# Routing into the experts of a hybrid layer: rows gathered without their norm, a weight slot as landing place, an embedding product cut in half groups, and a shorter overflow handler

## The chip, the cores and the metric

The kernel runs on one core of one Trainium2 chip. The time of a run is the device time in microseconds (us) of that core; runs are compared by their median. TensorE is called PE in the rows, VectorE DVE, ScalarE ACT, GpSimd POOL, and the queue of SyncE, which issues nearly all transfers, SP.

## The reference

One decoder layer on 512 tokens of width 1,024, all in float32. What matters here is its second half:

```python
x = x + hybrid_mixer(rms_norm(x, g_mix), ...)          # x1 in this text
h = rms_norm(x, g_moe)                                 # x1 * rstd * g_moe
# hier_moe(h): best of 4 groups, then the best 2 of its 4 experts
for e in range(16):
    hid = silu(t @ w_gate[e]) * (t @ w_up[e])          # t = h, 1024 -> 512
    y = y + combine[:, e:e + 1] * (hid @ w_down[e])    # 512 -> 1024
x = x + y
x = x + sigmoid(rms_norm(x, g_ple) @ w_ple_gate) * (p @ w_ple_proj)
```

Each expert has three float32 matrices of 2 MB. `p @ w_ple_proj` is the embedding; it depends on nothing that the layer computes, so it can be done anywhere before the end.

## The kernel before

Matrix products are taken in three parts: weights and activations are each split into a high part `hi` (ACT casts it) and a low part `lo` (DVE subtracts), and PE adds up hi·hi, hi·lo and lo·hi. A class `Stream` feeds the weights: loads of 1 MB go to "slots" (tags `raw0` to `raw4`, six more in `ringb`, and `x0`, `x1`, which first hold the residual stream), each slot is split in two steps into one of six pairs of hi/lo tiles, and a slot whose second half has been split is handed back (`W.give`), whereupon SP issues the next load into it. So SP runs ahead of PE by as many loads as there are free slots.

The experts work on gathered rows. Every expert has room for CAP = 96 tokens. In the last part of the mixer (`out_proj(t, 1)`, for four blocks `t` of 128 tokens) each block is squared (`square0`, `square1`), POOL raises the mean to the power -1/2 (`rs_moe`), DVE writes `h2 = x1 * rstd * g_moe` (`norm_moe`, L862), and SP stores it to the DRAM tensor `h2d` (L864). Router logits are made on PE from the transposed x1 (`x1_tr`, `logits`), compared on DVE (`route`), and turned into a place in each expert's list by a product with a triangular matrix (`rank`). A product of the one-hot matrix with `vals` (`slots`) gives the list of token numbers `toki`, the rows for the result `rowi` and the weights `sw`. For experts 0 and 1 this is done in two steps, first the list (columns 0 and 1 of `vals`), later the weight (columns 2 to 4, three bfloat16 parts of one float32), since the weights take longer (`weights`, `weights2`).

Then POOL gathers the rows of expert 0 into `xe[0]` and of expert 1 into `xe[1]` by an indirect transfer out of `h2d` (`gather`, L1060); PE transposes them (`transposed`, L1078), ACT and DVE split them (L1069, L1070), and the stream of expert products starts (`stream_mm`, `mm3`, L1103): for each expert gate (`pg`), up (`pu`) and down (`pd`). `silu` (L1125) and `times_up` (L1145) stand between them. The result rows are scaled by `sw` and added to the DRAM tensor `xd` by an indirect transfer (`scatter`, L1117).

The embedding is worked off beside the routing: eight groups `ple(i)` of six matmuls each (L804), with a copy out by ACT (`ple_out`, L812), are put by hand between the routing's steps. Order on each engine is the order of the program. Groups 0 to 2 lie before the gather, 3 to 5 behind it, 6 and 7 behind the transposes of expert 0.

After the gate product of expert 0 stands `overflow`: each engine loads the size of the fullest expert into a register (L1152) and jumps over a handler if it is at most 96 (L1153). With these inputs the handler is never entered. Its code is a loop over the 16 experts, with the 5 further portions of 96 tokens written out one after the other inside it.

Lines in the rows: L98 is the load of a weight slot by SP, L112 and L113 are `hi` and `lo` of `Stream.split`, L875 the logits' scaling, L917 the product in `slots`, L922 `toki`, L962 to L973 `weights2`.

Of the kernel before, what the change touches and what calls it, by code (L numbers as in the profile page):

```python
# [151 lines left out]
def hymba_layer(ctx, tc, x, p, g_mix, w_in, w_gla_gate, b_gla_gate, g_gla_out, w_conv, w_out,  # L152
# [18 lines left out]
    h2d = dram.tile([S, D], F32, name="h2d")  # L171
# [41 lines left out]
    vals = consts.tile([P, NT, NE, 5], BF16, name="vals")  # L213
# [60 lines left out]
    rows = mc.tile([P, P], F32, name="rows")  # L274
# [519 lines left out]
    def ple(i):  # L794

        t, ci = divmod(i, 2)
        if i == 0:
            for _ in range(2):
                wp.extend(W.take())
        pps_[i] = pp = mm_ps(f"pp{t}_{ci}")  # L800
        for k in range(2):
            (xh, xl), (wh, wl) = pT[k], wp[k]
            for n, (a, b_) in enumerate(((xh, wh), (xh, wl), (xl, wh))):
                pe.matmul(pp, a[:, tok(t)], b_[:, half(ci)], start=(k + n == 0), stop=(k == 1 and n == 2))  # L804
        if i == 7:
            W.done(2)
            W.give(pTt[0][0])
# [30 lines left out]
    x1T, h2, s2m, rs_moe = {}, {}, {}, {}  # L838
# [29 lines left out]
    def logits(t, ks=range(NK)):  # L868
# [5 lines left out]
        if NK - 1 in ks:  # L874
            ve.scalar_tensor_tensor(lg[:, t, :], pl[:, :20], rs_moe[t], brt, op0=OP.mult, op1=OP.add)  # L875
# [32 lines left out]
    sw = rtp.tile([CAP, NE], F32, name="sw", bufs=1)  # L908
# [3 lines left out]
    def slots(e, oh, vals, toki, rowi, sw, name, c0=0, c1=5, fill=False):  # L912
# [13 lines left out]
        if c1 == 5:  # L926
# [154 lines left out]
    for e in range(2):  # L1081
        gather(xe[e][:CAP], col(toki, e))
# [377 lines left out]
```

## Time and profile before

| | |
|---|---|
| median of three runs (lowest, highest) | 628.27 us (627.46, 628.48) |
| the profiled execution's own time | 629.62 us |
| its span, from first to last instruction | 627.9 us |
| mean granted clock of TensorE | 0.982 |
| busy: PE, DVE, ACT, POOL | 95%, 76%, 58%, 19% |
| DMA, mean over the span | 236 GB/s |

All positions below are us from the start of the span. The time lies 1.7 us over the span; the profiled execution is 1.35 us slower than the median. A PE that is reported busy is not a PE at its peak, since its matmuls overlap.

### The profile page before, as it was taken

Reading aid. Unit: us, or ns where it says so; the run is one execution under the profiler, and the core shown is the slowest. Engines: PE = TensorE matmul, PEld = TensorE weight load, DVE = VectorE, ACT = ScalarE, POOL = GpSimd, SP = SyncE. Lnnn points to the kernel's source line nnn. Section 1 sums busy time; section 2 is a strip of 40 time slices with the busy share of each in tenths; the row PEclk is TensorE's granted clock in tenths of the full one; section 3 lists DMA queues with packets and bytes.
Section 4 is the critical chain, followed back from the end, with each engine's and each line's share of the span. In section 5 each row is a group of like instructions: output and inputs, shape, how many; then the busy total and the mean of one; then the engine's idle time right before and its main releaser. Section 6 shows DMA issues by size and latency. Waiting matters only on the chain.

```text
span 627.9 us, 8404 instructions
## 1 busy us (share of the span) xinstructions
PE 594.7 (95%) x3006; PEld 453.8 (72%) x3006; DVE 479.6 (76%) x808; ACT 364.6 (58%) x516; POOL 121.9 (19%) x148
## 2 busy tenths in 40 slices
PE   7999999999999999559999999999999999988995
PEld 6897888887778787447777777777777777656784
DVE  4643799863593668359999999999999988879863
ACT  4532646103732342438788798777887977776332
POOL 1440654000700002002222222112222210100012
PEclk8999999999999999779999999999999999999998
DMA  8622221240129685776999999999999999986001
GB/s 274 207 102 68 101 68 67 68 135 1 67 68 331 239 316 224 256 264 234 356 356 353 368 368 356 354 354 350 354 347 362 367 340 363 369 256 260 34 34 67
DMA packets 73007, 148.45 MB, mean 236 GB/s; under 512 B 4797, under 2 KB 5396, under 8 KB 72942
## 3 DMA queue, kind: packets, MB, share of 16 engines
q1 hardware_dynamic: 69054, 136.69, 60.8%
q0 software_dynamic: 3744, 10.89, 7.6%
q8 instruction: 26, 0.43, 0.3%
q10 hardware_dynamic: 160, 0.27, 0.1%
q14 instruction: 23, 0.19, 0.1%
HBM read 137.56 MB, written 12.71 MB: 239 GB/s over the span
## 4 chain that ended last, share of the span: by engine, by line
PE 43%; DMA 6%; DVE 3%; ACT 2%; issue 1%; POOLq 0%; DVEq 0%; ACTq 0%
PE pu L1103 12%; PE pd L1103 11%; PE pg L1103 11%; PE pgate L1103 5%; DMA raw<-in_w_exp_down_dram 3%; DMA x<-in_w_exp_down_dram 2%; DMA x<-in_w_exp_up_dram 2%; DVE lo L113 1%; PE pt_xT L1078 1%; ACT hi L112 1%; PE pgate_last L1413 1%; DVE lo L118 1%; PE pt_hT L1078 1%; PE px L1310 1%; PE pz L1229 0%
## 5 line engine op out<-in xcount | busy, mean ns | idle before, releaser
L113 DVE TENSOR_TENSOR lo<-raw,hi 128x1024 fp32r<-128x1024 f32 x172 | 204.1, 1218 | 21.5 <-ACT hi L112 20.3
L112 ACT CAST hi<-raw 128x1024 fp32r<-128x1024 f32 x172 | 171.7, 1049 | 6.2 <-DMA raw<-in_w_exp_down_dram 4.9
L1060 POOL DMA_INDIRECT xe<-h2d,toki x16 | 27.9, 1741 | 200.9 <-PE pt_xT L1078 160.4
L118 DVE SCALAR_TENSOR_TENSOR lo<-raw,cst,hi 128x512 fp32r<-128x512 f32 (+1 forms) x52 | 41.9, 850 | 17.9 <-ACT hi L117 17.7
L113 DVE TENSOR_TENSOR lo<-x,hi 128x1024 fp32r<-128x1024 f32 x30 | 36.2, 1219 | 5.7 <-ACT hi L112 5.6
L1117 POOL DMA_INDIRECT xd<-ye,rowi x15 | 29.9, 1992 | 51.0 <-ACT ye L1271 47.4
L117 ACT ACTIVATE hi<-raw,cst 128x512 fp32r<-128x512 f32 (+1 forms) x52 | 34.0, 717 | 0.7 <-DMA raw<-in_w_in_dram 0.7
L112 ACT CAST hi<-x 128x1024 fp32r<-128x1024 f32 x30 | 30.9, 1050 | 2.1 <-DMA x<-in_w_exp_down_dram 1.8
L1103 PE MATMUL pg<-hi,xT_1h 128*96 128x512 f32 x60 | 24.5, 408 | 0.0
L1103 PE MATMUL pu<-hi,xT_0h 128*96 128x512 f32 x60 | 24.4, 407 | 0.0
L1103 PE MATMUL pu<-lo,xT_1h 128*96 128x512 f32 x60 | 23.8, 396 | 0.0
L1103 PE MATMUL pg<-hi,xT_1l 128*96 128x512 f32 x60 | 23.8, 396 | 0.0
L1103 PE MATMUL pu<-hi,xT_0l 128*96 128x512 f32 x60 | 23.8, 396 | 0.0
L1103 PE MATMUL pu<-hi,xT_1l 128*96 128x512 f32 x60 | 23.8, 396 | 0.0
L1103 PE MATMUL pg<-lo,xT_1h 128*96 128x512 f32 x60 | 23.7, 395 | 0.0
L1103 PE MATMUL pg<-hi,xT_0h 128*96 128x512 f32 x60 | 23.7, 395 | 0.0
L1103 PE MATMUL pg<-lo,xT_0h 128*96 128x512 f32 x60 | 23.7, 395 | 0.0
L1103 PE MATMUL pu<-lo,xT_0h 128*96 128x512 f32 x60 | 23.7, 395 | 0.0
L1103 PE MATMUL pg<-hi,xT_0l 128*96 128x512 f32 x60 | 23.7, 394 | 0.0
L1103 PE MATMUL pu<-hi,xT_1h 128*96 128x512 f32 x60 | 23.7, 394 | 0.0
L728 POOL TENSOR_TENSOR xs<-xs,sg 128x128 f32<-128x128 f32 x16 | 11.3, 736 | 44.2 <-ACT sg L723 44.1
L636 ACT ACTIVATE sq<-xs 128x512 f32<-128x512 f32 x4 | 2.5, 632 | 28.5 <-DVE xs L618 28.5
(539 smaller groups left out, 1583.9 us busy)
## 6 DMA issues: line engine op xcount, KB each, us to landing
raw<-in_w_exp_gate_dram SPq DMA_DIRECT2D x30, 1024.0 KB, 12.8
raw<-in_w_exp_down_dram SPq DMA_DIRECT2D x26, 1024.0 KB, 9.9
raw<-in_w_exp_up_dram SPq DMA_DIRECT2D x25, 1024.0 KB, 15.3
raw<-in_w_in_dram SPq DMA_DIRECT2D x10, 1024.0 KB, 5.1
x<-in_w_exp_up_dram SPq DMA_DIRECT2D x7, 1024.0 KB
x<-in_w_exp_down_dram SPq DMA_DIRECT2D x6, 1024.0 KB, 17.2
xs<-in_x_dram SPq DMA_DIRECT2D x16, 256.0 KB, 5.4
raw<-in_w_out_dram SPq DMA_DIRECT2D x4, 1024.0 KB
```

Source lines behind the costliest of these rows:

```text
L112: self.nc.scalar.copy(hi, rw)
L113: los.append(lambda: eng.tensor_sub(lo, rw, hi.bitcast(F32)))
L117: self.nc.scalar.activation(hi[:, c_], rw[:, c_], AF.Copy, scale=g_)
L118: los.append(lambda c_=c_, g_=g_: eng.scalar_tensor_tensor(lo[:, c_], rw[:, c_], g_, hi[:, c_].bitcast(F32), op0=OP.mult, op1=OP.subtract))
L636: se.activation(osq[c], to[c], AF.Square)
L728: ge.tensor_tensor(tv, tv, sgs[i][:, tok(t)], op=OP.mult)
L1060: ge.indirect_dma_start(out=x_, out_offset=None, in_=h2d, in_offset=bass.IndirectOffsetOnAxis(ap=idx, axis=0), bounds_check=S - 1, oob_is_ ...
L1078: pe.transpose(pt[:, k * n:(k + 1) * n], src[:n, tok(k)], ident[:n, :n])
L1103: pe.matmul(dst, a, b_, start=(k + n == 0), stop=(k == nk - 1 and n == 2))
L1117: ge.indirect_dma_start(out=xd, out_offset=bass.IndirectOffsetOnAxis(ap=idx, axis=0), in_=y_, in_offset=None, bounds_check=S + P - 1, oob_ ...
L1310: pe.transpose(pt[:, tok(k)], X(t)[:, ci * HALF + k * P:ci * HALF + (k + 1) * P], ident)
L1413: pe.matmul(pgl[i][:, :256], a, b_[:, 256 * i:256 * i + 256], start=(k + n == 0), stop=(k == NK - 1 and n == 2))
```

## The change

Five things. (1) The rows stored for the gather are `x1 * g_moe` without the reciprocal root (`gained`, into `xgd`), so they need no square, no power and no norm; they are stored one half row block at a time, the first half while the mixer still runs. The reciprocal root goes along as three more bfloat16 columns of `vals` (`norms`), comes out of `slots` as `sw[:, e, 1]`, and is applied in `silu` (its scale) and `times_up` (now a scalar_tensor_tensor). (2) Expert 0's rows land in the weight slot `x0`, which is handed back after they have been transposed; `x1` alone is freed beforehand. (3) The embedding runs in 16 half groups of three matmuls; 0 to 6 lie before the lists of tokens, 7 to 10 behind the gathers, 11 to 15 before the transposes, which therefore come after the whole embedding and, on DVE, after `norms` and `weights2`. (4) The lists of experts 2 and 3 are clamped as those of 0 and 1 were (`fill`), so that all 96 rows are gathered. (5) In the handler the 5 portions become an inner loop.

```diff
-    h2d = dram.tile([S, D], F32, name="h2d")
+    xgd = dram.tile([S, D], F32, name="xgd")
-    vals = consts.tile([P, NT, NE, 5], BF16, name="vals")
+    vals = consts.tile([P, NT, NE, 8], BF16, name="vals")
...
-    def ple(i):
-
+    def ple(j):
+
+        i, k = divmod(j, 2)
         t, ci = divmod(i, 2)
...
+        if k == 0:
+            pps_[i] = mm_ps(f"pp{t}_{ci}")
+        (xh, xl), (wh, wl) = pT[k], wp[k]
+        for n, (a, b_) in enumerate(((xh, wh), (xh, wl), (xl, wh))):
+            pe.matmul(pps_[i], a[:, tok(t)], b_[:, half(ci)], start=(k + n == 0), stop=(k == 1 and n == 2))
+        if k:
+            ple_out(i)
...
-    def norm_moe(t):
-        for i in range(2):
-            ve.scalar_tensor_tensor(h2[t][i], X(t)[:, half(i)], rs_moe[t], gmoe[:, half(i)],
-                                    op0=OP.mult, op1=OP.mult)
-            sy.dma_start(h2d[tok(t), half(i)], h2[t][i])
+        ge.tensor_tensor(rsm[:, t:t + 1], m, neghalf, op=OP.pow)
+
+    def gained(t, i):
...
+        ve.tensor_mul(xg[t, i], X(t)[:, half(i)], gmoe[:, half(i)])
+        sy.dma_start(xgd[tok(t), half(i)], xg[t, i])
...
+    def norms():
+
+        r3 = rtp.tile([P, NT, 3], BF16, name="r3", bufs=1)
+        for j in range(3):
+            ve.tensor_copy(r3[:, :, j], rsm)
+            if j < 2:
+                ve.tensor_tensor(rsm, rsm, r3[:, :, j], op=OP.subtract)
+        ve.tensor_copy(vals[:, :, :, 5:8], r3[:, :, None, :].to_broadcast([P, NT, NE, 3]))
...
     lo0 = W.split(later=True)
+    ple(0)
     x1_tr(t, 1)
     square1(t)
-    lo0()
-    ple(0)
-    norm_moe(t)
+    gained(t, 1)
     for u in range(2, NT):
         sy.dma_start(xd[tok(u)], X(u))
+    lo0()
+    ple(1)
+    ple(2)
     logits(t, range(4, NK))
     lo1 = W.split(later=True)
-    ple(1)
-    ple_out(0)
-    ple(2)
+    for j in range(3, 6):
+        ple(j)
     route(t)
-    ple_out(1)
     rank(t)
+    ple(6)
+    for e in range(2):
+        slots(e, oh01[e], vals, toki, rowi, sw, f"{e}", 0, 2, fill=True)
...
-    for e in range(2):
-        gather(xe[e][:CAP], col(toki, e))
-    W.free += [(ring, f"x{i}") for i in range(2)]
+
+    x0 = ring.tile([P, 2 * D], F32, tag="x0", name="xe_0")
+    gather(x0[:CAP, :D], col(toki, 0))
+    gather(xe[1][:CAP], col(toki, 1))
+    W.free.append((ring, "x1"))
     W.load()
-    for i in range(3, 6):
-        ple(i)
+    for j in range(7, 11):
+        ple(j)
     weights()
-    for i in range(3, 6):
-        ple_out(i)
     se.preload_act_table_set("silu_and_others")
+    norms()
     lo2()
-    xT = transposed(xe[0][:, half(0)], "xT0a") + transposed(xe[0][:, half(1)], "xT0b")
-    for i in range(6, 8):
-        ple(i)
-        ple_out(i)
     weights2()
+    for j in range(11, 16):
+        ple(j)
+    xT = transposed(x0[:, half(0)], "xT0a") + transposed(x0[:, half(1)], "xT0b")
+    W.give((ring, "x0"))
...
-        se.activation(sgs[e][:CAP], pgs[e][:CAP], AF.Silu)
+        se.activation(sgs[e][:CAP], pgs[e][:CAP], AF.Silu, scale=sw[:, e, 1:2])
...
-            slots(e, oh[e], vals, toki, rowi, sw, f"{e}")
+            slots(e, oh[e], vals, toki, rowi, sw, f"{e}", fill=(e < 4))
...
-        ve.tensor_mul(sgs[e][:CAP], sgs[e][:CAP], pus[e][:CAP])
+        ve.scalar_tensor_tensor(sgs[e][:CAP], pus[e][:CAP], sw[:, e, 1:2], sgs[e][:CAP], op0=OP.mult, op1=OP.mult)
...
-                for rep in range(1, -(-S // CAP)):
-                    kb = rt.tile([P, NT], F32, name="kb")
-                    ve.tensor_scalar(kb, ke, float(-CAP * rep), None, op0=OP.add)
+                with tc.For_i(1, -(-S // CAP), 1):
+                    ve.tensor_scalar(ke, ke, float(-CAP), None, op0=OP.add)
...
+    def first_weights():
+        for e in range(2):
+            slots(e, oh01[e], vals, toki, rowi, sw, f"{e}", 2, 8)
...
-    stream_mm(pgs[0][:CAP], xTs[0], NK, {3: lambda: silu(0)})
-    for e in range(2):
-        slots(e, oh01[e], vals, toki, rowi, sw, f"{e}", 2, 5)
+    stream_mm(pgs[0][:CAP], xTs[0], NK, {2: first_weights, 3: lambda: silu(0)})
```

## Rows read from the trace of the kernel before

**Rows 1.** Chain that ended last, in order of time (start, length, what)

```profile
285.73 2.85 PE pg L1103 x12
...
321.74 2.79 PE pg L1103 x12
...
489.99 17.53 DMA raw<-in_w_exp_down_dram
```

**Rows 2.** Windows: stretch, length, busy time of engines, PEclk, DMA share, GB/s

```profile
240.00:252.00 12.00, 10.73 (x64) 8.53 (x64) 10.55 (x36) 5.24 (x10) 4.33 (x3) 1.00 0.62 239
252.00:262.00 10.00, 3.65 (x15) 3.15 (x15) 2.22 (x9) 3.01 (x5) 0.00 (x0) 0.76 1.03 334
262.00:268.00 6.00, 6.00 (x24) 4.34 (x23) 3.19 (x8) 3.88 (x5) 0.00 (x0) 0.83 0.44 148
268.00:276.00 8.00, 2.55 (x18) 1.80 (x16) 4.97 (x10) 3.65 (x5) 0.00 (x0) 0.89 1.04 382
276.00:288.00 12.00, 10.92 (x51) 7.76 (x52) 6.76 (x19) 4.75 (x6) 1.93 (x1) 0.79 0.31 101
288.00:300.00 12.00, 12.00 (x64) 8.62 (x63) 11.63 (x20) 10.00 (x14) 4.70 (x2) 1.00 0.91 321
...
360.00:480.00 120.00, 120.00 (x592) 85.20 (x592) 112.54 (x160) 98.02 (x122) 23.84 (x13) 1.00 1.05 356
...
540.00:570.00 30.00, 26.41 (x115) 16.80 (x114) 22.53 (x25) 19.71 (x26) 1.41 (x1) 1.00 0.92 318
```

**Rows 3.** Timeline, 245 to 265 us: start, length, instructions, [idle before <-releaser]

```profile
247.64 0.15 DVE L922 TENSOR_SCALAR toki<-sv 96x1 int32<-96x1 f32 x1
...
248.84 1.86 POOL L1060 DMA_INDIRECT xe<-h2d,toki  x1 [5.56 <-DVE cmaxi L935]
...
249.71 0.38 SPq L98 DMA_DIRECT2D raw<-in_w_exp_up_dram  x1
...
258.37 0.90 PE L1078 MATMUL pt_xT0a<-ident,xe 96*128 96x96 f32 x4 [6.35 <-DMA xe<-h2d,toki]
...
264.50 0.40 PE L1103 MATMUL pg<-hi,xT0ah 128*96 128x512 f32 x1
```

**Rows 4.** Transfers out of h2d (16 gathers), view of the tensor

```profile
DMA to landing us min/median/max: 5.0/7.9/9.5
```

**Rows 5.** Timeline of DVE, 243 to 266 us

```profile
243.31 1.41 DVE L862 SCALAR_TENSOR_TENSOR h<-xs,rsmoe,gmoe 128x512 f32<-128x512 f32 x2 [0.44 <-POOL rsmoe L858]
244.64 0.23 DVE L875 SCALAR_TENSOR_TENSOR lg<-plog,rsmoe,brt 128x20 f32<-128x20 f32 x1
...
250.99 1.26 DVE L113 TENSOR_TENSOR lo<-raw,hi 128x1024 fp32r<-128x1024 f32 x1
259.82 0.56 DVE L1070 TENSOR_TENSOR xT0al<-pt_xT0a,xT0ah 128x384 fp32r<-128x384 f32 x1 [7.56 <-ACT xT0ah L1069]
...
260.93 0.16 DVE L962 TENSOR_REDUCE z__2396<-d__2342 128x4 f32<-128x16 f32 x1
...
263.38 0.26 DVE L971 CAST vals<-c__2347 128x64 bf16<-128x64 f32 x1
```

**Rows 6.** Instructions of the jump over the handler, by sequencer (ns min/median/max)

```profile
L1153 PEldq COMPARE_BRANCH  x2: 95/3190/6284, 268.4 to 270.7; - x2
...
L1153 SPq COMPARE_BRANCH  x2: 38/46/53, 274.4 to 280.4; - x2
```

**Rows 7.** Timeline of PE around the handler

```profile
270.06 0.48 PE L917 MATMUL pslot<-vals,oh 128*96 128x3 bf16 x8
277.08 0.74 PE L1103 MATMUL pu<-hi,xT0ah 128*96 128x512 f32 x1 [6.53 <-issue]
```

**Rows 8.** Page, part 3: the DMA queue that fetches code

```profile
q8 instruction: 26, 0.43, 0.3%
```

**Rows 9.** Instructions of lines L1145 and L1231

```profile
L1145 DVE TENSOR_TENSOR sg<-sg,pu x16: 675/676/684, 286.8 to 556.3; 96x512 f32<-96x512 f32 x16
...
L1231 DVE SCALAR_TENSOR_TENSOR raw<-pz,cwl,raw x8: 739/744/751, 565.1 to 590.9; 128x512 f32<-128x512 f32 x8
```

More of the change, by code (lines that the diff above doesn't have):

```diff
@@ L273, in hymba_layer @@
     load_x(0)
-    rows = mc.tile([P, P], F32, name="rows")
+    rows = t2k("rows")[:, :P]
     wg = mc.tile([RANK, 256], F32, name="wg")
@@ L792, in hymba_layer @@
     pps_ = {}
-    def ple(i):
+    def ple(j):
+        i, k = divmod(j, 2)
         t, ci = divmod(i, 2)
[L797 to L805, printed above, removed]
+        if j < 2:
+            wp.extend(W.take())
+        if k == 0:
[5 more added lines that the diff above has]
+            ple_out(i)
+        if j == 15:
             W.done(2)
@@ L836, in out_proj @@
         ve.tensor_add(xv, xv, pp)
-    x1T, h2, s2m, rs_moe = {}, {}, {}, {}
+    x1T, xg, s2m = {}, {}, {}
+    junk = [t2k(f"junk{i}") for i in range(2)]
+    rsm = rtp.tile([P, NT], F32, name="rsm", bufs=1)
     def x1_tr(t, i):
@@ L847, in square0 @@
     def square0(t):
-        h2[t] = h2[0] if t == 3 else [t2k(f"h2_{t}_{i}") for i in range(2)]
         s2m[t] = small.tile([P, 2], F32, tag="s2", name=f"s2moe{t}")
-        se.activation(h2[t][0], X(t)[:, half(0)], AF.Square, scale=D ** -0.5, accum_out=s2m[t][:, 0:1])
+        se.activation(junk[0], X(t)[:, half(0)], AF.Square, scale=D ** -0.5, accum_out=s2m[t][:, 0:1])
     def square1(t):
         v = X(t)[:, half(1)]
-        ve.scalar_tensor_tensor(h2[t][1], v, 1.0 / D, v, op0=OP.mult, op1=OP.mult, accum_out=s2m[t][:, 1:2])
+        ve.scalar_tensor_tensor(junk[1], v, 1.0 / D, v, op0=OP.mult, op1=OP.mult, accum_out=s2m[t][:, 1:2])
         m = small.tile([P, 1], F32, tag="ms", name=f"msmoe{t}")
         ve.scalar_tensor_tensor(m, s2m[t][:, 0:1], EPS, s2m[t][:, 1:2], op0=OP.add, op1=OP.add)
-        rs_moe[t] = small.tile([P, 1], F32, tag="rstd", name=f"rsmoe{t}")
-        ge.tensor_tensor(rs_moe[t], m, neghalf, op=OP.pow)
-    def norm_moe(t):
-        for i in range(2):
-            ve.scalar_tensor_tensor(h2[t][i], X(t)[:, half(i)], rs_moe[t], gmoe[:, half(i)],
-                                    op0=OP.mult, op1=OP.mult)
-            sy.dma_start(h2d[tok(t), half(i)], h2[t][i])
+        ge.tensor_tensor(rsm[:, t:t + 1], m, neghalf, op=OP.pow)
+    def gained(t, i):
+        if t < 2:
+            xg[t, i] = t2k(f"xg{t}_{i}")
+        else:
+            xg[t, i] = xg[t - 2, i]
+        ve.tensor_mul(xg[t, i], X(t)[:, half(i)], gmoe[:, half(i)])
+        sy.dma_start(xgd[tok(t), half(i)], xg[t, i])
     plog = {}
@@ L989, in hymba_layer @@
     for t in range(NT):
-        at = {1: lambda: (square0(t), x1_tr(t, 0))}
+        at = {1: lambda: (square0(t), x1_tr(t, 0), gained(t, 0))}
         if t:
@@ L993, in hymba_layer @@
             at[3] = lambda: logits(t - 1)
-            at[4] = lambda: (route(t - 1), norm_moe(t - 1))
+            at[4] = lambda: (route(t - 1), gained(t - 1, 1))
             at[6] = lambda: rank(t - 1)
@@ L1059, in gather @@
     def gather(x_, idx):
-        ge.indirect_dma_start(out=x_, out_offset=None, in_=h2d,
+        ge.indirect_dma_start(out=x_, out_offset=None, in_=xgd,
                               in_offset=bass.IndirectOffsetOnAxis(ap=idx, axis=0),
@@ L1188, in overflow @@
                     product(puv[:CAP], xv, w_exp_up, 0, [wa])
-                    se.activation(sv, pgv[:CAP], AF.Silu)
-                    ve.tensor_mul(sv, sv, puv[:CAP])
+                    se.activation(sv, pgv[:CAP], AF.Silu, scale=wv[:, 0, 1:2])
+                    ve.scalar_tensor_tensor(sv, puv[:CAP], wv[:, 0, 1:2], sv, op0=OP.mult, op1=OP.mult)
                     turned(hv, sv)
```

26 lines of the change are left out of this document (12 added, 14 removed).

## The prediction, made before the changed kernel ran

> **What bounds the kernel now.** I read the chain that ended last first. Followed back from the end it is the tail, then from 490 us on mostly waits for weight loads, the longest of 17.5 us [rows 1], and before that PE without a break back to 277 us. In between PE has a steady beat: gate products start at 285.73 and, two experts later, at 321.74, so 18.0 us for an expert [rows 1]. An expert's loads are six of 1 MB (1.05 million bytes); at the 356 GB/s of the full stretch [rows 2] each takes 2.94 us, so 17.7 us, and the gather and the scatter of up to 96 rows of 4 KB come on top (0.4 million bytes each at most, 1.1 us): 18.8 to 19.9 us. So DMA is the slower of the two by 1 to 2 us an expert, PE lives on the slots loaded ahead, and at 490 us they are used up. Read next the DMA share by stretch [rows 2]: 1.04 or 1.05 is full. It is full in the long stretch from 360 us on, and between 252 and 262 and 268 and 276 us, but not elsewhere. The end can come earlier only as far as DMA's idle time before 300 us goes away and as PE starts earlier; the smaller of the two counts.
>
> **DMA's idle time**, length times (1 - share / 1.04) [rows 2]: 240 to 252: 4.8 us; 252 to 262: 0.1; 262 to 268: 3.5; 276 to 288: 8.4; 288 to 300: 1.5. That is 18.3, of which 13.5 behind 252 us. In that stretch the slots were full: SP loads as DVE hands slots back, and DVE runs at most six half slots ahead of PE.
>
> **PE's two stalls.** PE runs out of work 6.35 us before 258.37, when the gathered rows have landed; the last twelve embedding matmuls come behind the transposes, and the experts start at 264.50 [rows 3]. [...] At 270.54 PE stops at the handler until 277.08, 6.54 us [rows 7]. Its jump alone took 6.28 us; the jump of SP took 0.05 [rows 6].
>
> **(1) and (3), up to the gather.** Before, the logits stood on DVE behind two norms that had waited for POOL: 243.31 + 1.41, logits at 244.64 [rows 5]. After, no norm is there, and the product on PE (behind three half groups instead of one group) sets them at about 243.9: 0.7 us earlier. Three half groups then hold PE's queue to 245.9, ahead of the rank product; so only 0.5 us is left at the list, which comes at 247.3 instead of 247.79. The gather started 1.05 us behind the list [rows 3]; the last normed rows were done at 244.72 (243.31 + 1.41) [rows 5] and had to be stored first, and I take that store for what it waited for. The new rows are stored some 2 us earlier, so the gather should start at 247.5, 1.3 us earlier. Its landing takes 5.0 to 9.5 us [rows 4]; before, it took the longest, because three loads were issued from 249.71 on [rows 3], while its descriptors were written until 250.70. Now they are written by 249.4, and two loads start then, the third having to wait for the slot x0. I take 6.3 us, nearer the low end: landing at 253.8; bounds 252.5 and 257.0.
>
> PE's cover for this wait: nine half groups of three matmuls, at the full-speed distance of 0.237 us (2.85 us for 12) [rows 1], 27 x 0.237 = 6.4 us from 247.6, to 254.0. So PE hardly idles and should keep its clock; with the landing at 257.0 it idles 3 us.
>
> DVE has more before the transposes now. `weights` ends at 251.0 as before, where `lo2` started, for the work ahead of it stays in place. Then come `norms`, five instructions on 4 columns (0.16 each, as the reduction at 260.93) and one copy of 192 elements (estimated at 0.4, from the 0.26 of a copy of 64), 1.2 us; `lo2`, 1.26; `weights2`, which took 260.93 to 263.64, 2.7; and the low part of the transposed rows, 0.56 [rows 5]. That ends at 256.7. PE's transposes (8 in some 0.7 us behind 254.0) and ACT's cast are done by 255.2. So DVE sets the start: the third matmul needs the low part, and two distances before it is 256.3. Gain of the experts' start: 264.5 - 256.3 = **8.2 us**. If the rows land at 257.0, transposes, cast and low part take the 2.0 us they took before (258.37 to 260.38), start 258.5 [rows 3, 5]: 6.0 us.
>
> **(5) The handler.** PE's code in one portion is 40 matmuls (4 for the list, 12 transposes, 24 products) with their weight loads, 80 instructions, so at least 400 before and about 80 after; SP has 24 loads a portion, 120 in all, and its jump over these took 0.05 us [rows 6]. After the change PE jumps less far than SP did before. Code is fetched by DMA in pieces of 0.43 MB / 26 = 16.5 KB [rows 8]; I read the 6.28 us as such a fetch, since nothing else is late. Bounds: 0.05 us (SP) and 6.28 (as before). I take 0.1, leaving a stall of 0.3: gain 6.2. Behind the stall the granted clock is 0.79 over 276 to 288 us [rows 2], and 277.08 to 285.73 is 8.65 us [rows 1, 7], against 24 matmuls of 0.237 and about 1.0 us of transposes and lists, 6.7: gain 2.0. Together **8.2 us** on PE. The weights for it lie ready: they were split before the stall.
>
> **(2) and (4), DMA.** With 16.4 us less on PE, slots are handed back that much earlier. The gather starts 1.3 us earlier, and of DMA's idle time ahead of it I count 1.0 as gained. From there, about 250.3, I follow the queue: two loads and two gathers (2.9 million bytes at 356 GB/s) to 258.4; x0's load is issued at 254.8; then the loads that follow the experts' start come 8.2 us earlier, those behind the handler 16 us. Each is issued before the one ahead of it has landed, so of the 13.5 us idle I leave 0.5. x0's later load costs nothing: its 2.9 us fill a gap. Clamping the lists of experts 2 and 3 gathers about 32 more rows each (1,024 places over 16 experts is 64 of 96): 0.26 million bytes, 0.7 us lost. Sum: 1.0 + 13.0 - 0.7 = **13.3 us**.
>
> **What costs nothing.** `times_up` becomes a scalar_tensor_tensor: 0.744 us on 128 rows against 0.676 [rows 9], 0.07 an expert on DVE, which is busy 112.5 of 120 us [rows 2]; hidden as long as the loads set the pace. Had DVE no such cover, 16 x 0.07 = 1.1 us. Six columns instead of three in the reduction of `slots`, a scale on `silu`: under 0.05 each, hidden alike. `first_weights` sits behind the third of four steps of gate 0; `silu(0)` waits for it perhaps 0.3 us, with three split half slots ready for PE.
>
> **The sum.** DMA gives 13.3, PE 16.4; the smaller counts: 13.3. The profiled 629.62 would become 616.3; from the median 628.27, **615.0 us**. PE would then starve sooner and about 3 us more than before.
>
> **The rivals.**
> A. *The handler's jump still misses* (code behind it not yet on the core). For it: no row shows PE jump a shorter way. Against it: SP's 0.05 us over 120 loads. PE keeps 8.2; DMA's gap at the handler stays but for x0's load and the shifted ones, some 7 us idle behind 252 instead of 0.5: gain 13.3 - 6.7 = 6.6, **621.7 us**.
> [...]
> B. *DMA cannot use the time*: only the gap at the handler closes (8.4 + 1.0 - 0.7), because slots come back no sooner elsewhere: 8.7, **619.6 us**. Against it: the loads hang on PE's start.
> C. *DMA does not bind*: the whole 16.4 of PE arrives, **611.9 us**. For it: PE is idle only 3.6 us between 540 and 570 [rows 2], so the two are close.
> D. *Slower*: the inner loop makes the way past the handler several fetches in series. The rest gains 6.6 with one fetch of 6.3, so from a passage of 12.9 us on nothing is left; three fetches are 18.8, and the kernel takes 628.3 + 5.9 = **634 us**. Against it: PE shows two jumps there, and one took 0.095 us [rows 6].
> E. *No change*: a passage of two fetches, 628.
>
> **How the numbers follow.** Forecast 0.66 (its own range 612.8 to 617.5, from a start 2 us later or DMA gaps of 0 to 2.5 us), C 0.08, B 0.10, A 0.11, D 0.03, E 0.02. The range runs from C to just beyond B, 611.8 to 620.4; it leaves out A, D, E and a bit. Faster by over 0.2% (1.3 us, about what can be told from no change): 0.95; within: 0.02; slower: 0.03.
>
> **What would show it.** The first gate matmul at 256 to 257; no PE gap above 3 us at the gather; PE's jump under 0.2 us and the up product at full clock; DMA share near 1.04 from 251 us on; the long waits for loads starting before 490 us. Wrong if the jump still takes 6 us, if POOL starts the gather no earlier, or if DMA shows gaps behind 260.

## The result and the profile after

The changed kernel took **621.42 us** (median of 4 runs, 620.28 to 621.88), the kernel before 627.87 us in the runs beside it: ratio 0.9896 (95% interval 0.9876 to 0.9915), so 6.5 us faster, about half of the 13.3 that were forecast. The profiled execution took 621.88 us with a span of 620.1, against 629.62 and 627.9. One run of all those told of here, one of `no_handler`, fell to a granted clock of 0.848 and took 658.88 us; it is left out of that kernel's figures.

Windows of the changed kernel over the stretches of [rows 2] (last three columns: granted clock, DMA share, GB/s):

```profile
240.00:252.00 12.00, 12.00 (x71) 9.78 (x70) 9.99 (x42) 8.01 (x13) 3.95 (x3) 1.00 0.51 200
252.00:262.00 10.00, 5.70 (x19) 3.82 (x18) 5.83 (x15) 4.86 (x8) 0.00 (x0) 0.70 1.03 347
262.00:268.00 6.00, 4.52 (x24) 2.85 (x22) 2.70 (x5) 2.00 (x3) 0.00 (x0) 0.93 1.05 397
268.00:276.00 8.00, 6.37 (x27) 4.45 (x28) 4.74 (x15) 2.44 (x4) 1.93 (x1) 0.79 0.52 188
276.00:288.00 12.00, 12.00 (x64) 8.58 (x63) 11.65 (x23) 9.42 (x13) 3.15 (x1) 1.00 0.76 243
288.00:300.00 12.00, 12.00 (x61) 8.62 (x60) 11.71 (x16) 9.64 (x13) 3.76 (x2) 1.00 1.05 341
```

By the prediction's formula DMA is idle 6.1 us before 252 and 7.2 behind it (4.0 in 268 to 276, 3.2 in 276 to 288), where it was 4.8 and 13.5: only 6.3 of the 13.5 came back. The clock is at 0.70 in the ten microseconds in which the rows of expert 0 arrive, and dips again behind the handler. The timeline of the changed kernel, to be laid beside [rows 3, 7]:

```profile
245.92 0.15 DVE L927 TENSOR_SCALAR toki<-sv 96x1 int32<-96x1 f32 x1
...
247.03 2.04 POOL L1074 DMA_INDIRECT xe<-xgd,toki  x1 [5.52 <-DVE cmaxi L940]
...
248.09 0.38 SPq L98 DMA_DIRECT2D raw<-in_w_exp_up_dram  x1
...
248.66 0.38 SPq L98 DMA_DIRECT2D x<-in_w_exp_up_dram  x1
...
256.71 0.90 PE L1092 MATMUL pt_xT0a<-ident,xe 96*128 96x96 f32 x4 [4.30 <-DMA xe<-xgd,toki]
...
258.18 0.74 PE L1118 MATMUL pg<-hi,xT0ah 128*96 128x512 f32 x1
258.72 0.63 PE L1118 MATMUL pg<-lo,xT0ah 128*96 128x512 f32 x1
259.15 0.63 PE L1118 MATMUL pg<-hi,xT0al 128*96 128x512 f32 x1
...
263.17 0.40 PE L1118 MATMUL pg<-hi,xT0bh 128*96 128x512 f32 x1
263.41 0.39 PE L1118 MATMUL pg<-lo,xT0bh 128*96 128x512 f32 x1
...
269.63 0.65 PE L1118 MATMUL pu<-hi,xT0ah 128*96 128x512 f32 x1 [3.12 <-ACT hi L112]
```

Three things are to be seen. The gather starts at 247.03, but its rows are there only 9.7 us later, and PE idles 4.3 us. The gate product then starts at half clock (0.50 from 256.7 to 260 us, 1.00 from 263 us on): its matmuls follow each other at 0.43 us, 4.7 us later at 0.24. And before the first up product PE stops for 3.12 us. The jump is not the cause of that. Here are the instructions at the jump by sequencer (ns min/median/max), then the timeline of ACT and DVE around it:

```profile
L1168 SPq EVENT_SEMAPHORE  x8: 17/17/17, 270.9 to 275.4; - x8
...
L1168 PEldq COMPARE_BRANCH  x2: 90/142/193, 264.3 to 266.7; - x2
...
L1168 SPq COMPARE_BRANCH  x2: 38/44/49, 270.7 to 275.5; - x2
...
L1168 DVEq EVENT_SEMAPHORE  x1: 21/21/21, 269.5 to 269.5; - x1
```

```profile
266.56 0.68 ACT L1140 ACTIVATE sg<-pg,sw 96x512 f32<-96x512 f32 x1 [4.00 <-PE pg L1118]
267.14 1.03 ACT L112 CAST hi<-raw 128x1024 fp32r<-128x1024 f32 x1
...
268.21 1.23 DVE L113 TENSOR_TENSOR lo<-raw,hi 128x1024 fp32r<-128x1024 f32 x1 [1.84 <-ACTq L1168]
```

PE jumps in 0.19 us, where it took 6.28 [rows 6]. But `silu(0)`, the `hi` and the `lo` of one more half slot stand in series ahead of the jump on ACT and DVE; DVE passes it at 269.5, and PE goes on at 269.63. PE's row names ACT's cast, which ends at 269.54, as what came last; that PE does not wait for ACT there is shown by `if_before_split` below.

The chain that ended last (start, length, what) is PE without a break from 269.63 to 546 us; four of its steps:

```profile
268.50 1.05 ACT hi L112
269.63 2.78 PE pu L1118 x6
...
303.45 2.85 PE pd L1118 x12
...
321.35 2.85 PE pd L1118 x12
```

The beat is 17.9 us, and no weight load is left in the chain; before, it went through several, one of 17.5 us [rows 1].

With times of PE out of the timelines, the profiled runs can be laid side by side; all in us, "hidden" is the first matmul that transposes an expert's hidden rows (`pt_hT`), "last" that of expert 15, "px" the first transpose behind it. "To landing" ends with the first transpose of expert 0's rows; in `filled` and `filled_split` PE was still at work then, so the rows may have been there earlier:

| run | gather starts | to landing | to gate 0 | to up 0 | to hidden 0 | hidden 0 to last | last to px | px to end | span |
|---|---|---|---|---|---|---|---|---|---|
| before | 248.84 | 9.53 | 6.13 | 12.58 | 11.34 | 268.62 | 8.87 | 61.99 | 627.9 |
| after | 247.03 | 9.68 | 1.47 | 11.45 | 11.09 | 266.38 | 9.98 | 63.02 | 620.1 |
| loop_alone | 247.88 | 10.13 | 5.51 | 7.39 | 10.82 | 269.47 | 8.86 | 63.14 | 623.2 |
| written_out | 246.90 | 9.48 | 1.47 | 13.74 | 11.39 | 266.36 | 8.87 | 61.89 | 620.1 |
| no_handler | 246.94 | 9.47 | 1.47 | 7.66 | 11.74 | 265.90 | 8.86 | 62.16 | 614.2 |
| if_before_split | 247.07 | 9.45 | 1.47 | 8.80 | 11.40 | 266.47 | 8.86 | 62.48 | 616.0 |
| filled | 247.10 | 9.42 | 1.06 | 9.45 | 10.89 | 266.50 | 9.92 | 63.06 | 617.4 |
| filled_split | 247.16 | 9.41 | 1.07 | 6.87 | 12.97 | 266.52 | 8.87 | 62.53 | 615.4 |
| x0_first | 247.16 | 5.62 | 1.12 | 10.27 | 11.07 | 268.02 | 8.86 | 62.38 | 614.5 |
| x0_first_split | 247.27 | 5.21 | 1.22 | 8.00 | 12.96 | 269.64 | 9.92 | 63.38 | 617.6 |
| x0_handler | 248.03 | 6.06 | 1.61 | 6.04 | 11.72 | 268.20 | 9.91 | 62.13 | 613.7 |
| x0_handler_one | 246.83 | 8.85 | 2.27 | 7.49 | 11.73 | 266.38 | 8.86 | 62.19 | 614.6 |
| handler_early | 247.74 | 9.55 | 1.44 | 8.23 | 11.73 | 266.37 | 8.86 | 62.48 | 616.4 |
| own_tile | 246.72 | 9.26 | 1.12 | 10.83 | 12.33 | 266.34 | 8.87 | 62.33 | 617.8 |
| loads_later | 247.31 | 9.60 | 1.47 | 11.49 | 11.07 | 266.35 | 8.87 | 63.04 | 619.2 |

A profiled run is one run, and not the median: the spans of before and after differ by 7.8 us, the medians by 6.5, and the profiled runs of `x0_first_split` and `x0_handler` are the slowest of their four.

### The profile page after: what moved, and what is told of

Same layout as the page of the kernel before. It is cut to its first block, busy times and chain, and to the rows that moved or that the text cites. A ratio compares the mean times of both kernels' runs of the same rounds, so it can differ in the third digit from the quotient of the medians.

```text
span 620.1 us, 8403 instructions
## 1 busy us (share of the span) xinstructions
PE 594.3 (96%) x3006; PEld 453.9 (73%) x3006; DVE 481.7 (78%) x814; ACT 366.1 (59%) x516; POOL 121.1 (20%) x148
## 3 DMA queue, kind: packets, MB, share of 16 engines
q0 software_dynamic: 3744, 11.09, 7.8%
## 4 chain that ended last, share of the span: by engine, by line
PE 53%; DVE 2%; ACT 1%; issue 0%; POOL 0%; DVEq 0%; ACTq 0%; POOLq 0%
PE pd L1118 15%; PE pu L1118 15%; PE pg L1118 13%; PE pgate L1118 5%; PE pt_xT L1092 2%; PE pgate_last L1429 1%; PE pt_hT L1092 1%; DVE lo L118 1%; PE px L1326 1%; DVE raw L1245 0%; PE pz L1243 0%; PE pslot L922 0%; ACT hi L112 0%; DVE sg L1160 0%; ACT hi L117 0%
## 5 line engine op out<-in xcount | busy, mean ns | idle before, releaser
L113 DVE TENSOR_TENSOR lo<-raw,hi 128x1024 fp32r<-128x1024 f32 x172 | 204.4, 1218 | 19.6 <-ACT hi L112 17.5
L1074 POOL DMA_INDIRECT xe<-xgd,toki x16 | 28.1, 1753 | 194.0 <-PE pt_xT L1092 159.6
L118 DVE SCALAR_TENSOR_TENSOR lo<-raw,cst,hi 128x512 fp32r<-128x512 f32 (+1 forms) x56 | 44.8, 843 | 17.7 <-ACT hi L117 17.5
L117 ACT ACTIVATE hi<-raw,cst 128x512 fp32r<-128x512 f32 (+1 forms) x56 | 36.7, 717 | 0.5 <-DMA raw<-in_w_in_dram 0.5
```

Of the source, the lines that this page charges most:

```text
L113: los.append(lambda: eng.tensor_sub(lo, rw, hi.bitcast(F32)))
L117: self.nc.scalar.activation(hi[:, c_], rw[:, c_], AF.Copy, scale=g_)
L118: los.append(lambda c_=c_, g_=g_: eng.scalar_tensor_tensor(lo[:, c_], rw[:, c_], g_, hi[:, c_].bitcast(F32), op0=OP.mult, op1=OP.subtract))
L1074: ge.indirect_dma_start(out=x_, out_offset=None, in_=xgd, in_offset=bass.IndirectOffsetOnAxis(ap=idx, axis=0), bounds_check=S - 1, oob_is_ ...
```

## The experiments

Ratios are to the kernel before, run beside each kernel on the same chip (its medians there: 627.4 to 629.0 us). Ratios, not microseconds, are compared between groups of runs; one hundredth is 6.3 us. Of the five edits only (2) and (5) were taken out by themselves; what (1), (3) and (4) are worth one by one was not separated.

**Each half of the change alone.** `loop_alone` puts edit 5 into the kernel before; `written_out` takes it out of the changed kernel.

```diff
-                for rep in range(1, -(-S // CAP)):
-                    kb = rt.tile([P, NT], F32, name="kb")
-                    ve.tensor_scalar(kb, ke, float(-CAP * rep), None, op0=OP.add)
+                with tc.For_i(1, -(-S // CAP), 1):
+                    ve.tensor_scalar(ke, ke, float(-CAP), None, op0=OP.add)
...
```

> The kernel before with the inner loop in the handler alone (edit 5). Theory (the jump was the long part of PE's stop, but under it lay another wait: PE may not go on before the engine that reads its PSUM buffer in the handler has passed the jump too): PE's jump falls from 6.28 to under 0.3 us, the stop before the first up product from 6.54 to between 1.3 and 3.1 us, and the kernel takes 623 to 625.5 us, since the gather's part of the gain is missing. Rival 1 (all of the gain measured is the loop's, the rest of the change gives nothing): 621.4. Rival 2 (the other wait is as long as the jump was): stop of 6 us, 627.9.

> The changed kernel with the five portions of the handler written out again (the change without edit 5). Theory (the jump comes back and takes PE's wait for DVE under itself): PE's jump 6.3 us, the stop before the first up product 6.5 instead of 3.1 us, 3 to 4 us slower than the changed kernel: 624.5 to 626 us where the kernel before takes 628. Rival 1 (all but edit 5 gains nothing in any case, as the kernel before with the loop alone was as fast as the whole change): 628. Rival 2 (the jump's time is set by what lies behind it, not by its length): stop of 3.1 us, 621.4.

`loop_alone`: 622.86 us, ratio 0.9901 (0.9885 to 0.9918). `written_out`: 622.68 us, ratio 0.9908 (0.9886 to 0.9930). Each half alone gains 6 us, both together 6.5. The stop before the first up product, in the timelines of `loop_alone` and `written_out`:

```profile
270.91 0.47 PE L1103 MATMUL pu<-hi,xT0ah 128*96 128x512 f32 x1 [1.34 <-ACTq L1153]
```

```profile
271.59 0.71 PE L1118 MATMUL pu<-hi,xT0ah 128*96 128x512 f32 x1 [5.63 <-issue]
```

In `loop_alone` PE waits for ACT to pass the jump (1.34 us); in the changed kernel for DVE, which comes later (3.12). In `written_out` the jump is back (5.27 us) and covers that wait. The up product starts at 277.08 before, and 270.91, 271.59 and 269.63 in the three; the two gains, 6.2 and 5.5, would add up to 265.4; in the next run, without any handler, it starts at 265.54. `written_out` was expected 3 to 4 us behind the changed kernel; it is 0.8 behind, since its up product is 1.96 us later, but in the profiles its last down product and its tail ran 1.1 us faster each. The first of these is a matter of the clock (see the end). The tail behind `px` takes 61.9 to 63.4 us in these 15 profiles, and nothing here shows why. Which edit turned the wait from ACT to DVE was not separated.

**The handler's place.** `no_handler` leaves the handler and its jump out; `if_before_split` only moves the jump by one split.

```diff
-    stream_mm(pgs[0][:CAP], xTs[0], NK, {2: first_weights, 3: lambda: silu(0)})
-    overflow(0)
+    stream_mm(pgs[0][:CAP], xTs[0], NK, {2: first_weights, 3: lambda: (silu(0), overflow(0))})
```

> The changed kernel without the handler and the jump over it (the handler is never entered with these inputs, so the same result is computed). Theory (the 3.1 us stop before the first up product is all the handler's, and PE sets the pace): no stop there, full clock in that product, 3.1 + about 1.4 us less: 616.9 us. Rival 1 (DMA has become the bound, as predicted): PE starts earlier but waits later for weights, at most 1.5 us are left: 620 or more. Rival 2 (PE waits there for the split of the eighth half slot for its own sake): the stop stays, 621.4.

> The changed kernel with the jump put ahead of the last split behind gate 0 (hi and lo of one more half slot now come behind it on ACT and DVE); nothing else differs. Theory (PE waits until DVE has passed the jump, which in the changed kernel stands behind silu, hi and lo in series): DVE passes some 2 us earlier, the stop falls from 3.1 to about 1.2 us and part of the half clock behind it goes: 618.5 to 619.5 us. Rival (the stop is a fetch of code or the jump itself): 3.1 us as before, 621.4.

`no_handler`: 615.91 us (three runs), ratio 0.9803 (0.9781 to 0.9825). `if_before_split`: 617.37 us, ratio 0.9813 (0.9795 to 0.9830), with this stop in its timeline:

```profile
266.79 0.44 PE L1118 MATMUL pu<-hi,xT0ah 128*96 128x512 f32 x1 [0.55 <-PEq L1168]
...
269.75 0.67 PE L922 MATMUL pslot<-vals,oh 128*96 128x8 bf16 x4 [1.35 <-DVE oh L1070]
```

and this passing of ACT among the instructions at the jump:

```profile
L1168 ACTq COMPARE_BRANCH  x2: 38/42/45, 266.8 to 267.1; - x2
```

The stop goes from 3.12 to 0.55 us without a change to the jump: it was the wait for DVE. DVE has passed at 266.2 here; ACT passes only at 267.1 and casts behind that, and PE goes on at 266.79, so it waits neither for ACT's passing nor for its cast. What comes out from under the stop is a next wait, 1.35 us for the list of expert 2, and 1.74 us in `no_handler`. Both gained more than expected; the table shows 3.4 and 2.5 us up to the first hidden transposes, and 1.1 us more in the last down product, which is the clock's (see the end).

**The landing of the rows.** `loads_later` and `x0_first` both hold the weight loads back in the program; the second also makes x0's slot, free only when PE has transposed the rows, the first to be loaded. The edit of `x0_first`:

```diff
     lo2 = W.split(later=True)
+    held_specs, W.specs = W.specs, []
     lo1()
...
-    W.give((ring, "x0"))
+    W.specs = held_specs
+    W.free.insert(0, (ring, "x0"))
+    W.load()
```

> The changed kernel with the two weight loads that were issued within a microsecond of the gather, and the one behind the embedding, held back until the rows of expert 0 have been transposed. Theory (the gathered rows land 9.7 us after issue because these loads share the transfer engines with them): the rows land about 5 us after issue, near 252; PE does not idle and keeps its clock, the experts start at 255 to 256 instead of 258.2, and with PE as the bound the kernel takes 616.5 to 618.5 us. Rival 1 (writing and fetching the descriptors, or the store of the rows, sets the landing): they land at 256 to 257 as now, and the kernel takes 621.4 or more. Rival 2 (DMA binds): the experts start at 255 to 256, but the 5 us in which no load runs come back as waits for weights later: 621.4 to 625.

> The changed kernel with x0, which comes free when the rows of expert 0 have been transposed, as the first slot to be loaded: the three loads that followed the gather now stand behind x0's on SP. In the run loads_later they kept their issue times of 248 to 252 us, since SP only waits for a slot, whatever the order of the program. Theory (the rows land 9.7 us after issue because these loads share the transfer engines with them): they land about 5 us after issue, PE idles less than 1 us, DVE's weights2 sets the experts' start at 255.5 to 256, at full clock; with PE as the bound 617 to 619 us. Rival 1 (descriptors or the store of the rows set the landing): rows at 256 to 257 as now, 621.4 or more. Rival 2 (DMA binds): start at 255.5 to 256, but the transfer time left empty comes back later: 621.4 to 625.

`loads_later`: 621.56 us, ratio 0.9884 (0.9867 to 0.9900), with the loads issued at 248.38 and 248.95 and the rows landing 9.6 us after the gather's start: nothing had been held back, so it tells only how well a run repeats. `x0_first`: 616.44 us, ratio 0.9810 (0.9787 to 0.9833). Its timelines of POOL, PE and ACT:

```profile
247.16 2.05 POOL L1075 DMA_INDIRECT xe<-xgd,toki  x1 [5.52 <-DVE cmaxi L940]
```

```profile
252.78 0.55 PE L1093 MATMUL pt_xT0a<-ident,xe 96*128 96x96 f32 x4 [0.24 <-DMA xe<-xgd,toki]
...
255.32 0.47 PE L1121 MATMUL pg<-hi,xT0al 128*96 128x512 f32 x1 [0.71 <-DVE xT0al L1085]
...
264.17 0.58 PE L1121 MATMUL pu<-hi,xT0ah 128*96 128x512 f32 x1 [3.12 <-ACT hi L112]
```

```profile
491.61 1.05 ACT L112 CAST hi<-raw 128x1024 fp32r<-128x1024 f32 x1 [3.75 <-DMA raw<-in_w_exp_down_dram]
```

Without a load beside them the rows land after 5.6 us. PE hardly idles (0.24 us ahead of the transposes), DVE sets the third gate matmul (255.32), the clock stays at 1.00 from 252 to 264 us, and the gate product runs at full speed, its matmuls 0.23 us apart. The stop at the handler is still 3.12 us, so the two losses are separate. And waits for loads are back: from the first hidden transposes to the last it takes 1.6 us longer than in the changed kernel. `own_tile` takes edit 2 out (both x0 and x1 loaded at once: three loads within 2.1 us of the gather's start), and `x0_handler_one`, which is told below, has one.

```diff
-    gather(x0[:CAP, :D], col(toki, 0))
+    gather(xe[0][:CAP], col(toki, 0))
...
-    W.free.append((ring, "x1"))
+    W.free += [(ring, f"x{i}") for i in range(2)]
```

> The changed kernel with expert 0's rows gathered into their own tile as before, x0 and x1 both handed over for loads at once (the change without its second edit): three loads instead of two are issued within 2 us of the gather. Theory (the rows land when the transfers issued beside them are through): the third load of 1 MB takes 2.9 us of the engines, so the rows land 1 to 3 us later than 256.6, the experts start that much later, and DMA is ahead by a load: 622 to 624 us. Rival (the landing hangs on the gather's own descriptors): lands as now, 621.4.

`own_tile`: 621.08 us, ratio 0.9902 (0.9885 to 0.9920), rows after 9.3 us. The expectation fell: a third load costs the gather nothing more, and edit 2 as made gives nothing.

**The clock.** `filled` keeps PE at work while it waits; `filled_split` adds the moved jump.

```diff
+    pdum = aux_ps("pdum")
+    for _ in range(18):
+        pe.matmul(pdum, pT[0][0][:, tok(0)], wp[0][0][:, half(0)], start=True, stop=True)
     xT = transposed(x0[:, half(0)], "xT0a") + transposed(x0[:, half(1)], "xT0b")
```

> The changed kernel with 18 further matmuls of 128x512 between the embedding and the transposes of expert 0, whose result nobody reads: they keep PE at work (18 x 0.237 = 4.3 us) while the gathered rows are on their way, and change nothing else. Theory (the 4.3 us idle costs PE its clock, and gate 0 then runs at half of it until 263): rows land as now at 256.5, the clock stays at 1.00 from 252 us on, gate 0 takes 5.7 instead of 8.3 us; about 2.5 us less: 618.9. Rival (the slow matmuls of gate 0 wait for their weights' split, not for the clock): as the changed kernel, 621.4. If the 18 matmuls outlast the landing, some tenths of a us come on top.

> The changed kernel with both: the 18 matmuls that only keep PE at work, and the jump ahead of the last split. Theory (two separate losses, PE the bound): what the two give alone adds up, about 2.5 + 4.8 = 7.3 us below the changed kernel: 614 us. Rival (DMA becomes the bound when PE is 4 us or more faster, as the prediction had it): waits for weight loads come back from 480 us on, and no more than 5.5 us are gained: 616 us or more.

`filled`: 619.49 us, ratio 0.9855 (0.9828 to 0.9882), 2.6 us below the changed kernel as expected. Its windows:

```profile
252.00:258.00 6.00, 5.76 (x31) 4.43 (x29) 2.94 (x12) 1.69 (x5) 0.00 (x0) 1.00 1.05 321
258.00:264.00 6.00, 5.91 (x32) 3.83 (x30) 5.45 (x8) 3.75 (x5) 0.00 (x0) 1.00 1.04 386
```

These 18 matmuls compute nothing, and the kernel is faster with them: the clock is 1.00 in both windows, where it was 0.70 from 252 to 262 us. `filled_split`: 617.20 us, ratio 0.9823 (0.9800 to 0.9846), no better than `if_before_split` alone; the theory (614) fell, and of the rival only the time came, without its waits for loads (266.52 us from hidden to last). PE is 2.3 us ahead of `if_before_split` at the first up product, and 0.7 at the hidden transposes. The chain of `filled_split` in between:

```profile
264.96 1.06 ACT hi L112
266.04 1.23 DVE lo L113
267.26 0.17 DVE oh L1070
267.48 0.67 PE pslot L922 x4
```

Behind the jump the product for expert 2's list waits 1.35 us for a one-hot matrix that stands on DVE behind the split. `if_before_split` has the same wait; what is lost here beyond it is the clock, which falls to 0.91 and 0.80 in the two windows of 6 us from 264 us on, where it stays at 1.00 there (matmuls 0.43 us apart from 269.0 to 272.2 instead of 0.23; 12.97 us from up to hidden instead of 11.40). Why it falls behind the same two waits in the one and not in the other stays open.

**Where DMA binds, and both repairs.** `x0_first_split` shortens the stop of `x0_first`; `x0_handler` instead puts handler and jump right behind the transposes of expert 0, ahead of the held loads; `handler_early` does it in the changed kernel, ahead of the transposes, with loads under way; `x0_handler_one` is `x0_handler` with one load issued at 247.90.

```diff
     xT = transposed(x0[:, half(0)], "xT0a") + transposed(x0[:, half(1)], "xT0b")
+    overflow(0)
+    W.specs = held_specs
+    W.free.insert(0, (ring, "x0"))
+    W.load()
```

> x0_first together with the jump ahead of the last split. In x0_first weight loads became late again (six waits of ACT for them between 491 and 530 us, 268.0 us from the first hidden transposes to the last, where the changed kernel takes 266.4). Theory (DMA is the bound from about 616 us down): PE reaches the up product some 2.6 us earlier, and gives it back as longer waits for loads; the stretch between these transposes grows to about 270, the time stays at 615.5 to 616.5. Rival (PE still sets the end): the 3 to 4 us that the same edit gave the changed kernel come in full, 613 us.

> x0_first with the handler and its jump ahead of the loads that were held back, right behind the transposes of expert 0. Theory (the handler costs twice: PE's wait for DVE, and a gap in DMA, because SP passes the jump only when all its loads have landed): here SP has no load on the way and DVE is behind weights2 anyhow, so the third gate matmul comes about 1 us later than in x0_first, but the stop of 3.1 us and the half clock behind it go, and DMA's share has no gap between 264 and 288 us (3 us of transfers): 612.5 to 614 us. Rival 1 (DMA binds and the gap is not the handler's): 616 or more. Rival 2 (the wait for DVE moves along and is as long here): 617 to 619.

> The changed kernel with the handler and its jump ahead of the transposes of expert 0, in the wait for the gathered rows; loads as in the changed kernel. Theory (in that wait the passage is covered): rows land at 256.5 as now, no stop before the up product, which starts at 265.5 as without the handler: 616 to 617 us. Rival 1 (SP passes the jump only when its loads have landed, which here holds back x0's and the next loads): waits for loads come back, 618 to 620. Rival 2 (the passage costs PE the same anywhere): 621.

> x0_handler, but with one of the held loads, that into the slot which the split ahead of the gather frees, issued as in the changed kernel some 1 us behind the gather's start. Without a load beside them the rows landed 5.6 us after issue, with two 9.7 us, with three 9.3 us. Theory A (transfers share the engines, so the gather's landing grows with the bytes beside it): with one load they land after 7 to 8 us; PE starts 1 to 2 us later than in x0_handler, DMA is a load of 2.9 us ahead, and as DMA sets the end the time is 611 to 613 us. Theory B (any load beside the gather holds it back by the same 4 us): they land after 9 us or more, PE idles 3 us and loses its clock: 615 to 617. Rival C (one load makes no difference to either): 613.

`x0_first_split`: 616.91 us, ratio 0.9831 (0.9810 to 0.9852). Its up product starts 2.5 us earlier than that of `x0_first`, its first hidden transposes 0.6, mostly since the wait of 1.35 us for expert 2's list comes out here too; then it takes 269.64 instead of 268.02 to the last ones, in waits for loads. Nothing is left of the gain: here DMA binds. Not all of that is the rate of the transfers: SP now comes to the jump at 263.0, ahead of the load that `x0_first` issued at 264.00, and issues none before 274.77; DMA's share is 0.49 in 270 to 276 us, where that of `x0_first` is 0.77. `x0_handler`: **613.15 us, ratio 0.9773 (0.9754 to 0.9791)**, the fastest of all, 1.2% below the changed kernel (its interval still overlaps a little with those of `no_handler`, `x0_first` and `x0_handler_one`). Its windows, and the longest wait for a load in its timeline of ACT:

```profile
258.00:264.00 6.00, 5.30 (x30) 3.45 (x28) 4.46 (x7) 3.83 (x5) 0.00 (x0) 1.00 1.02 380
264.00:270.00 6.00, 4.97 (x29) 3.70 (x30) 5.26 (x16) 2.68 (x5) 1.93 (x1) 1.00 1.05 399
270.00:276.00 6.00, 6.00 (x33) 4.30 (x32) 5.92 (x15) 4.58 (x6) 2.39 (x1) 1.00 1.04 338
276.00:288.00 12.00, 12.00 (x62) 8.55 (x61) 11.68 (x16) 11.04 (x15) 4.52 (x3) 1.00 1.05 387
```

```profile
489.87 1.05 ACT L112 CAST hi<-raw 128x1024 fp32r<-128x1024 f32 x1 [3.97 <-DMA raw<-in_w_exp_down_dram]
```

Clock and DMA share are full from 258 us on. In the changed kernel SP sits at the jump from 270.7 to 275.5 us, with eight semaphore instructions in between, and DMA's share is 0.37 from 273 to 276; here it comes to the jump with no load under way and is through in 0.7 us. But the DMA gap was the handler's only in part. Windows of `no_handler`:

```profile
270.00:276.00 6.00, 6.00 (x36) 4.35 (x35) 5.52 (x11) 4.35 (x6) 1.08 (x1) 1.00 0.79 257
276.00:282.00 6.00, 6.00 (x34) 4.26 (x33) 5.97 (x14) 4.19 (x6) 3.15 (x1) 1.00 0.71 270
```

By the prediction's formula DMA is idle there for 4.3 us between 264 and 288 us, without any handler, and for 7.3 in the changed kernel: some 3 us are the handler's. In `x0_handler` the loads held back fill the rest, after a share of only 0.55 from 252 to 258 us.

`handler_early`: 617.41 us, ratio 0.9841 (0.9823 to 0.9859). PE has no stop before the up product, but SP issues no load from 253.5 to 265.0, and DMA's share is 0.73 and 0.60 in the two windows of 6 us from 258 us on. The time lies between its theory (616 to 617) and its first rival (618 to 620). The rival's waits for loads did not come back: from hidden to last it takes 266.37 us, as in the changed kernel. Its span is 2.2 us longer than that of `no_handler`, by 0.8 in the gather's start, 0.6 in gate 0 and 0.8 behind the hidden transposes of expert 0, so no cost of the DMA gap is shown in this run. `x0_handler_one`: 616.62 us, ratio 0.9810 (0.9776 to 0.9843), theory B: the gather starts at 246.83, and in the timeline of PE

```profile
255.68 0.90 PE L1093 MATMUL pt_xT0a<-ident,xe 96*128 96x96 f32 x4 [3.48 <-DMA xe<-xgd,toki]
```

the rows come after 8.85 us, PE idles 3.5 us, and the clock is 0.69 and 0.74 in the windows of 6 us from 252 us on. A single load beside the gather costs most of what three cost (9.3 to 10.1 us to landing, against 5.2 to 6.0 with none).

## Why the prediction was wrong

The direction and the size of PE's jump were right, the time lay just outside the range. The forecast took the smaller of two sums: DMA's 13.3 us and PE's 16.4. PE's came to 7.7 at the first hidden transposes and set the end. By the table's columns:

- **Gather's start**: forecast 1.3 us earlier; 1.81 in the two profiles, but 0.96 of that is not the change's: `loop_alone`, the same program up to there, starts at 247.88. The granted clock was 0.91 in the first 20 us of the profile of before and 1.00 there. So 0.85. The store of the rows, which the prediction took for what the gather waited for, was not it: the gather follows its list by 1.05 us before and by 0.96 after, and what came earlier was the list, by 0.76 against `loop_alone` instead of 0.5. That the number came near is luck.
- **"I take 6.3 us, nearer the low end"** for the landing: this step failed. It was 9.7, above the upper bound taken. The reason given, one load fewer beside the gather, was wrong: with one load it is 8.85, with two 9.4 to 9.7, with three 9.3 to 10.1 (`own_tile`, before, `loop_alone`), and only with none 5.2 to 6.0. Nor did the two loads wait for the end of POOL's instruction (249.4 in the prediction, 249.07 measured): they were issued at 248.09 and 248.66. That descriptors are written in it, as the prediction has it, is the author's reading; no view shows it. And the 5.0 us at the low end of [rows 4] were no ordinary case: they are the one gather that fell into the DMA gap behind the handler (share 0.31 [rows 2]), here in the timeline of before with its landing; the 15 others took 7.5 us or more.

```profile
281.42 1.93 POOL L1060 DMA_INDIRECT xe<-h2d,toki  x1 [29.44 <-DVE oh L1056]
...
DMA to landing us min/median/max: 5.0/5.0/5.0
```

The start of gate 0 was 258.18, as worked out for a late landing (258.5), so 6.3 us were gained there instead of 8.2.
- **"PE hardly idles and should keep its clock"** hung on that step, and the late case was priced without the clock. Gate 0 took 8.3 us, from 258.18 to the end of its last matmul at 266.5, instead of the 6.0 of before (264.50 to 270.54), where the last twelve embedding matmuls had run at half clock first (0.54 from 258.37 to 264.50). 2.3 us lost, of which `filled` gave back 2.0 (257.58 to 263.9). Moving the embedding ahead of the transposes took away work that had absorbed the slow stretch.
- **The jump**: forecast 0.1 us, measured 0.19, and as much in `loop_alone` (6.28 before, 5.27 in `written_out`): in these four runs the short handler is cheap to jump over and the long one is not. That the long jump waits for a fetch of code is the author's reading of [rows 8]. The views of DMA fit it and do not prove it: queue q8, named "instruction" on the page, moves one piece of 0.02 MB in the long stop of before (270.5 to 277.1 us) and none in the shorter one of the changed kernel (266.4 to 269.7). One came in the changed kernel between 262 and 266.4 us too, where PE did not stop. For which engine a piece is, they do not say.
- **"Leaving a stall of 0.3"**: the second step that failed. Under the jump lay a wait of PE for DVE to pass it, 3.12 us now; nothing of it showed while the jump was longer. 3.4 us were gained instead of 6.2, and 0.25 instead of 2.0 behind it, since the stop again cost the clock (0.79 in 268 to 276 us).
- **"Of the 13.5 us idle I leave 0.5"**: DMA's sum failed too. 7.2 us stayed idle, and 1.3 more than before came ahead of 252 us, where 1.0 was to be gained. SP's hold at the jump was in the prediction's own rows: its two jump instructions, of 0.05 us each, start at 274.4 and 280.4 [rows 6], and the prediction read only their lengths.
- **"The smaller counts: 13.3"**: PE set the end, with less than half of its forecast; no load is left in the chain. DMA bound less than the prediction read from "the longest of 17.5 us" [rows 1]: that is the length of a load in the chain, during which PE worked on, and what the waits for loads cost PE before is some 2.2 us (268.62 against 266.38 from hidden to last). That DMA binds a little further down was right: 1.6 us of waits in `x0_first`, and in `x0_first_split` what was left of a shorter stop.
- The remaining terms: the waits for loads that went away gave 2.2 us (268.62 to 266.38); the last down product and the tail took 1.1 and 1.0 us more, neither shown to be the change's. 7.7 + 2.2 - 2.1 = 7.8, the difference of the spans.
- `times_up` measured 0.74 us, as forecast, and costs nothing: the beat is 17.9 us. `silu` with its scale took 0.69 us against 0.60, 0.09 more, where the prediction allowed 0.05.

Rival A's 621.7 is the time measured, but by another mechanism, which makes that luck: its jump would still have missed. C named the bound rightly, PE, but with all of its 16.4 us.

## What to carry to other kernels

Jumps of 6.28 and 5.27 us hid waits of 1.34 and 3.12 at the same place here (before, `written_out`): before the removal of a long delay is priced, list what each engine behind it waits for, what stands ahead of those engines at the jump, and what an idle PE costs in clock afterwards (2.0 us in the gate product here). The small gather on the critical path of this kernel landed 4 us earlier with no bulk load beside it (5.6 against 9.7 us), and an order in the program didn't ensure that (`loads_later`, 9.6 us); a dependence did (`x0_first`). In the fastest version (`x0_handler`, 613.15 us) the jump over rarely used code stands where no transfer was under way, SP passing in 0.7 us, and where the engines that PE waits for pass it beside other work, 0.73 us of waiting for ACT being left.

## What the runs showed of the hardware

- The indirect gather of expert 0's rows (0.4 MB) landed 5.2 to 6.0 us after its start with no load beside it (the gather of expert 1 follows in all runs), 8.85 with one load of 1 MB issued about 1 us behind it, 9.4 to 9.7 with two, 9.3 to 10.1 with three. A single load held it back by some 3 us, and two more by at most 1.3 beyond that.
- SP took 4.8 us to pass the jump with loads under way (270.7 to 275.5), 4.9 with a single one (`x0_handler_one`, 249.2 to 254.1), and 0.7 with none (first row, `x0_handler`). In `handler_early` the last load ahead of the jump was issued at 253.14 and landed 11.1 us later, at 264.2 (second row); the last of SP's semaphore instructions at the jump is at 264.3 (third row). So SP passed there when that load had landed.

```profile
L1119 SPq COMPARE_BRANCH  x2: 38/46/53, 248.8 to 249.5; - x2
```

```profile
raw<-in_w_exp_gate_dram SPq DMA_DIRECT2D x1, 1024.0 KB, 11.1
```

```profile
L1117 SPq EVENT_SEMAPHORE  x8: 17/17/17, 254.5 to 264.3; - x8
```

- The same two stops ahead of the last down product (0.84 and 0.57 us) were followed by full clock in `loads_later`, with matmuls mostly 0.23 us apart, and by about half of it in the changed kernel, with 0.43 from 550.96 to 552.24. Windows of the changed kernel, then of `loads_later`, which issues the same work in the same order:

```profile
550.00:555.00 5.00, 5.00 (x17) 3.16 (x16) 4.56 (x6) 4.06 (x7) 0.00 (x0) 0.70 1.01 381
```

```profile
550.00:555.00 5.00, 4.79 (x21) 3.04 (x19) 4.76 (x6) 4.32 (x8) 0.00 (x0) 1.00 0.98 323
```

It costs 1.1 us (9.98 against 8.87 from `last` to `px`), in 4 of the 15 profiles of this study. What decides it stays open; it bounds how finely two versions of this kernel can be told apart by one profile.
